# Cross-attention over a memory: one pass over both streams in place of two, with split operands kept in DRAM

## The chip, the cores and the metric

The kernel runs on one core of a Trainium2 chip. The metric is device time in microseconds (us) of one execution. TensorE (PE) does matmuls, VectorE (DVE) and ScalarE (ACT) the elementwise work, GpSimd (POOL) a little of it, and SyncE (SP) issues most DMAs; ACT issues some. SP and ACT each have a DMA queue, and each engine works through its own instructions in order.

## The reference, cut to what matters

```python
D_MODEL = 1024; SEQ = 256; DEC_SEQ = 512; N_MEM = 256; XA_HEADS = 4; XA_HEAD_DIM = 256

def memory_cross_attention(x, mem, w_q, w_kv, w_o):
    B, T, _ = x.shape
    M = mem.shape[1]
    q = (x @ w_q).reshape(B, T, XA_HEADS, XA_HEAD_DIM)
    k, v = jnp.split(mem @ w_kv, 2, axis=-1)
    k = k.reshape(B, M, XA_HEADS, XA_HEAD_DIM)
    v = v.reshape(B, M, XA_HEADS, XA_HEAD_DIM)
    s = jnp.einsum('bthd,bmhd->bhtm', q, k).astype(jnp.float32) * (XA_HEAD_DIM ** -0.5)
    p = jax.nn.softmax(s, axis=-1).astype(v.dtype)
    o = jnp.einsum('bhtm,bmhd->bthd', p, v).reshape(B, T, D_MODEL)
    return o @ w_o
# one layer: x = LN0(a*x + 0.5*SwiGLU_1(x)); x = LN1(a*x + mixer(x));
#            x = LN2(a*x + memory_cross_attention(x, mem)); x = LN3(a*x + 0.5*SwiGLU_2(x))
```

It is done for two streams with the same weights: S ("sample"), 512 tokens, and P ("prompt"), 256 tokens, each with a memory of its own of 256 rows.

## The kernel before

All arithmetic is float32. Every operand of a matmul is split into a high and a low part (`split`: ACT copies the source to `hi`, DVE computes `lo = src - hi`), and a product is three matmuls: hi x hi, hi x lo, lo x hi. `load_w` brings 128 x 1024 of a weight into one of three `raw` buffers by SP's queue and splits it into one of five `wh`/`wl` pairs.

The stages are: first feed-forward, mixer, cross-attention, second feed-forward. The mixer ends with the merge: products with w_gla_out (`pt<-oT,wh`), gated and added up on DVE (`sig`, `t`), and split into `xh`/`xl`. Then `tok_out` multiplies with w_mix_out, 48 matmuls of 512 columns (`to`) for two token tiles and one half of the columns, and adds into `acc`, the residual in SBUF (128 x 6 token tiles x 1024); `norm` is the layer norm on DVE; `to_T` transposes `acc` on PE (`lt`) and splits it into `xh`/`xl`.

Cross-attention is done stream after stream by a `Cross` object, with 33 buffers of 128 x 512 ("units"). `keys_values` is a generator; `fill(ns)` takes steps from it between the `to_T` calls and `drain` takes the rest. K has 256 columns a matmul (one stream), V 512. `attend` goes through the heads: the query projections (`pt<-xh,wh`, 512 columns for S and 256 for P) stand between the scores (`sc`), softmax (`mx`, `e`, `sm`), transposes of the probabilities (`pT`) and the products with V (`ov`). `project` multiplies with w_xo. The weights w_xk, w_xv, w_xq and w_xo are loaded and split for each stream.

The feed-forwards use seven products in place of eight for a pair of weight blocks (`seven`, `products`): the input is held as quarters A11 to A22 and sums S1 to S4 of them (`sums`, on DVE), the weight blocks are summed too, and each of the seven products has 12 matmuls of 384 columns, in the accumulators `px`, `py`, `pz`.

A scheduler places what the Python code records: engines' queues come out in an order of its own, within what buffers and pools allow. A tile's buffers are set by `bufs`; a load into a buffer waits until its last reader is done.

Of the kernel before, what the change touches and what calls it, by code (L numbers as in the profile page):

```python
# [14 lines left out]
D = 1024  # L15
NK = 8
# [8 lines left out]
UNITS = 33  # L25
WARM = 8
LO_K = (5, 7)
LO_V = (1, 3)
# [5 lines left out]
FILL = (14000, 14000, 8000, 14000)  # L34
# [24 lines left out]
def _encoder(ctx, tc, nc, io, out, dbg):  # L59
# [30 lines left out]
    def load_w(src, lo_eng=None, pool=None, in_parts=False):  # L90

        raw = wp.tile([128, 1024], F32, tag="raw", bufs=3, name=nid("raw"))
        h = (pool or wp).tile([128, 1024], F32R, tag="wh", bufs=1 if pool else 5, name=nid("wh"))
        l = (pool or wp).tile([128, 1024], F32R, tag="wl", bufs=1 if pool else 5, name=nid("wl"))
# [963 lines left out]
    def tok_out(src, groups, lhs, after, alt=False, hooks=()):  # L1058


        hooks = list(hooks)
        for half in range(2):
            ws = []
            for gi, (s, ts) in enumerate(groups):
                pss = [psum(nid("to")) for _ in ts]
                for kp in range(4):
                    if gi == 0:
                        ws.append(load_w(src[kp, half], nc.vector if alt and kp % 2 else None))
                    for x, t in enumerate(ts):
                        tcs = slice(t * 128, (t + 1) * 128)  # L1070
                        for kk in range(2):
                            k = 2 * kp + kk
                            lh, ll = lhs(s, k, tcs)
                            tok_mm(pss[x][:], ws[kp], kk, lh, ll, k == 0, k == NK - 1)
                    if hooks:
                        hooks.pop(0)()
                for x, t in enumerate(ts):
                    add_acc(s, t, half, pss[x][:], True)
                if half == 1:
                    after[gi]()  # L1080
# [5 lines left out]
    class Cross:  # L1086
        def __init__(self, s, ap, bufs):
            self.s, self.ap, self.bufs = s, ap, bufs
            self.Kt, self.V, self.q, self.sc, self.pr, self.oT = [], {}, {}, {}, {}, []

        def unit(self, name, dt=F32R):
            return self.ap.tile([128, 512], dt, tag="u", bufs=self.bufs, name=nid(name))

        def load_mem(self, pin):
            s, unit = self.s, self.unit
            self.mh, self.ml = [], []
            raws = [unit("mraw", F32) for c in range(4)]
            for c in range(4):
                if pin:
                    tc.keep_in_program_order(nc.scalar.dma_start(raws[c][:], io[f"mem{s.name}"][c]))  # L1100
                else:
                    nc.sync.dma_start(raws[c][:], io[f"mem{s.name}"][c])
            for c in range(4):
                a, l = unit("mh"), unit("ml")
                split(a[:], l[:], raws[c][:])
                self.mh += [a[:, 0:256], a[:, 256:512]]
                self.ml += [l[:, 0:256], l[:, 256:512]]

        def keys_values(self):
            s, unit, mh, ml = self.s, self.unit, self.mh, self.ml  # L1110
            for h in range(4):
                ps = psum(nid("K"))
                for b in range(2):
                    w = load_w(io["w_xk"][2 * h + b], nc.vector if (2 * h + b) in LO_K else None)
                    proj_T(w, s, rh=mh, rl=ml, T=256, ps=ps[:, b * 256:(b + 1) * 256])
                    yield 2650
                a, l = unit("Kh"), unit("Kl")
                split(a[:], l[:], ps[:])
                self.Kt.append((a, l))
            for half in range(2):  # L1120
                pss = [psum(nid("V")) for _ in range(2)]
                for kp in range(4):
                    w = load_w(io["w_xv"][kp, half], nc.vector if kp in LO_V else None)
                    for m in range(2):
                        for kk in range(2):
                            k = 2 * kp + kk
                            ms = slice(m * 128, (m + 1) * 128)
                            tok_mm(pss[m][:], w, kk, mh[k][:, ms], ml[k][:, ms], k == 0, k == NK - 1)
                    yield 2600
                for m in range(2):  # L1130
                    a, l = unit("Vh"), unit("Vl")
                    split(a[:], l[:], pss[m][:])
                    self.V[m, half] = (a, l)

        def query(self, h, b):
            s = self.s
            w = load_w(io["w_xq"][2 * h + b], nc.vector if b and s is P else None)
            ps = proj_T(w, s)
            a, l = self.unit("qh"), self.unit("ql")
            split(a[:, :s.T], l[:, :s.T], ps)  # L1140
            self.q[h, b] = (a, l)

        def scores(self, h):
            s = self.s
            kh, kl = self.Kt[h]
            es = []
            for tp in range(s.nt // 2):
                ps = psum(nid("sc"))
                for u in range(2):
                    tcs = slice((2 * tp + u) * 128, (2 * tp + u + 1) * 128)  # L1150
                    for b in range(2):
                        bs = slice(b * 256, (b + 1) * 256)
                        qh, ql = self.q[h, b]
                        mm3(ps[:, u * 256:(u + 1) * 256], qh[:, tcs], ql[:, tcs], kh[:, bs], kl[:, bs],
                            b == 0, b == 1)
                mx = sp.tile([128, 2], F32, tag="mx", name=nid("mx"))
                sm = sp.tile([128, 2], F32, tag="sm", name=nid("sm"))
                nc.vector.tensor_reduce(mx[:], ps[:].rearrange("p (a b) -> p a b", b=256), AX.X, ALU.max)
                nc.vector.tensor_scalar(mx[:], mx[:], -1.0 / 16, None, ALU.mult)
                e = self.unit("e", F32)  # L1160
# [4 lines left out]
                nc.vector.reciprocal(sm[:], sm[:])  # L1165
                for u in range(2):
                    us = slice(u * 256, (u + 1) * 256)
                    nc.vector.tensor_scalar(e[:, us], e[:, us], sm[:, u:u + 1], None, ALU.mult)
                es.append(e)
            self.sc[h] = es  # L1170

        def probs_T(self, h):
            s = self.s
            pr = []
            for m in range(2):
                ps = psum(nid("pT"))
                for t in range(s.nt):
                    c = (t % 2) * 256 + m * 128
                    nc.tensor.transpose(ps[:, t * 128:(t + 1) * 128], self.sc[h][t // 2][:, c:c + 128], ident[:])
                a, l = self.unit("ph"), self.unit("pl")  # L1180
                split(a[:, :s.T], l[:, :s.T], ps[:, :s.T])
                pr.append((a, l))
            self.pr[h] = pr

        def values(self, h):
            s = self.s
            for b in range(2):
                ps = psum(nid("ov"))[:, :s.T]
                es = slice((h % 2) * 256 + b * 128, (h % 2) * 256 + (b + 1) * 128)
                for m in range(2):  # L1190
                    vh, vl = self.V[m, h // 2]
                    ph, pl = self.pr[h][m]
                    mm3(ps, vh[:, es], vl[:, es], ph[:, :s.T], pl[:, :s.T], m == 0, m == 1)
                a, l = self.unit("oh"), self.unit("ol")
                split(a[:, :s.T], l[:, :s.T], ps)
                self.oT.append((a, l))

        def attend(self):
            self.query(0, 0)
            self.query(0, 1)  # L1200
            self.query(1, 0)
            for h in range(4):
                self.scores(h)
                if h < 3:
                    self.query(h + 1, 1)
                if h > 0:
                    self.values(h - 1)
                if h == 0:
                    self.query(2, 0)
                if h < 3:  # L1210
                    self.probs_T(h)
                if h == 1:
                    self.query(3, 0)

        def project(self, after):
            groups = [(self.s, ts) for ts in ((0, 1), (2, 3))[:self.s.nt // 2]]
            tok_out(io["w_xo"], groups, lambda s, k, tcs: (self.oT[k][0][:, tcs], self.oT[k][1][:, tcs]),
                    after, self.s is P, [lambda: self.probs_T(3), lambda: self.values(3)])
# [234 lines left out]
```

## Time and profile before

| | |
|---|---|
| median of 3 timed runs | 1767.03 us (1766.86 to 1767.19) |
| profiled execution | 1769.73 us, span 1767.9 us |
| mean granted clock of PE | 0.997 |
| PE / DVE / ACT / POOL busy | 1756.3 / 1259.6 / 764.4 / 26.0 us |
| DMA | 253.11 MB, mean 143 GB/s |
| first w_mix_out matmul | at 932.27 us |
| first weight of S's K | at 999.25 us |
| last matmul of the old attention | about 1268 us |

The profiled execution took 2.7 us longer than the median of the timed ones; sums are made against it, and then carried to the median. In rows of groups the columns are: line, engine, operation, output <- inputs, shapes and count, then busy time in us, mean duration in ns, and the idle time before them with what ended it. In rows of the order of time: start, duration, engine, line, operation. PE's matmuls overlap, so the time that one takes from the stream is the distance between two starts and not its duration. In rows of a window: window, length, busy us of PE, weight loads, DVE, ACT and POOL, granted clock, DMA share, GB/s. Line numbers are those of the kernel before.

### The profile page before, as it was taken

The page shows a single profiled execution, that of the slowest core. Times are in us where ns is not written, and L with a number is a line of the kernel's source. Part 1 is how long each engine was busy: PE and PEld are TensorE (multiplying, and loading weights), DVE is VectorE, ACT ScalarE, POOL GpSimd, SP SyncE. Part 2 cuts the span into 40 slices and gives each one's busy share as a digit, 9 for nine tenths or more (in the row PEclk, how much of TensorE's full clock was granted, in tenths as well). Part 3 has the DMA queues.
Part 4 walks back from the last instruction along what each step waited for, and adds up shares of the span by engine and source line. Part 5 has one row for each costly group of instructions (what it writes and reads, how often), then busy time and mean ns, then how long its engine had stood idle before and what let it go on. Part 6 is the DMA issues. An engine that isn't in the chain of part 4 may idle for free.

```text
span 1767.9 us, 25206 instructions
## 1 busy us (share of the span) xinstructions
PE 1756.3 (99%) x9758; PEld 1617.2 (91%) x9758; DVE 1259.6 (71%) x2151; ACT 764.4 (43%) x1291; POOL 26.0 (1%) x60
## 2 busy tenths in 40 slices
PE   9999999999999999999999999999999999999998
PEld 9999999988899999888888988899899999998886
DVE  8777777687668554678675965596697777766866
ACT  6444444443235544655232253345344444444431
POOL 0000000000100000000000000000000000000002
PEclk9999999999999999999999999999999999999999
DMA  5433333587333334211364262255423333337951
GB/s 198 141 120 118 123 123 112 203 312 262 134 108 108 132 125 131 95 48 49 116 218 131 83 191 72 84 191 167 155 80 127 114 124 125 129 100 288 336 181 72
DMA packets 100536, 253.11 MB, mean 143 GB/s; under 512 B 10017, under 2 KB 28193, under 8 KB 100417
## 3 DMA queue, kind: packets, MB, share of 16 engines
q1 hardware_dynamic: 92352, 234.73, 39.4%
q10 hardware_dynamic: 8064, 16.78, 2.6%
q8 instruction: 76, 1.25, 0.3%
q14 instruction: 44, 0.35, 0.1%
HBM read 205.07 MB, written 46.40 MB: 142 GB/s over the span
## 4 chain that ended last, share of the span: by engine, by line
PE 96%; DVE 2%; DMA 1%; ACT 0%; issue 0%; SPq 0%; DVEq 0%; ACTq 0%
PE px L475 23%; PE dn L286 13%; PE py L475 11%; PE pz L475 6%; PE pt L106 6%; PE pt L107 6%; PE pt L108 6%; PE to L106 2%; PE to L107 2%; PE to L108 2%; PE dn L107 2%; PE dn L106 2%; PE dn L108 2%; PE pp L475 1%; PE lt L191 1%; PE K L108 1%
## 5 line engine op out<-in xcount | busy, mean ns | idle before, releaser
L87 ACT ACTIVATE wh<-raw 128x512 fp32r<-128x512 f32 (+2 forms) x309 | 256.1, 831 | 314.3 <-PE pt L107 77.5
L88 DVE TENSOR_TENSOR wl<-raw,wh 128x512 fp32r<-128x512 f32 (+2 forms) x309 | 289.1, 938 | 142.6 <-ACT wh L87 141.9
L286 PE MATMUL dn<-wh,ao 128*128 128x512 f32 x600 | 185.5, 389 | 0.0
L106 PE MATMUL pt<-xh,wh 128*128 128x512 f32 (+2 forms) x512 | 173.8, 339 | 0.0
L107 PE MATMUL pt<-xl,wh 128*128 128x512 f32 (+2 forms) x512 | 173.2, 338 | 0.0
L108 PE MATMUL pt<-xh,wl 128*128 128x512 f32 (+2 forms) x512 | 172.7, 337 | 0.0
L286 PEld LDWEIGHTS dn<-wh,ao 128*128 128x128 f32 x600 | 112.6, 188 | 23.5
L87 ACT ACTIVATE wh<-tt 128x512 fp32r<-128x512 f32 x156 | 94.0, 624 | 72.0 <-PE px L475 60.5
L286 PE MATMUL dn<-wl,ao 128*128 128x512 f32 x300 | 116.7, 389 | 0.0
L106 PEld LDWEIGHTS pt<-xh,wh 128*128 128x128 f32 x512 | 97.4, 190 | 9.9 <-issue 0.5
L88 DVE TENSOR_TENSOR wl<-tt,wh 128x512 fp32r<-128x512 f32 x156 | 104.0, 685 | 3.0 <-ACT wh L87 2.2
L107 PEld LDWEIGHTS pt<-xl,wh 128*128 128x128 f32 x512 | 97.6, 191 | 9.0 <-issue 0.3
L108 PEld LDWEIGHTS pt<-xh,wl 128*128 128x128 f32 x512 | 97.5, 190 | 9.1
L552 DVE SCALAR_TENSOR_TENSOR h<-sil,sum 128x384 f32<-128x384 f32 x78 | 43.5, 557 | 54.8 <-ACT sil L551 54.8
L475 PE MATMUL px<-xh,wl 128*128 128x384 f32 x232 | 77.5, 334 | 0.0
L475 PE MATMUL px<-xh,wh 128*128 128x384 f32 x232 | 77.5, 334 | 0.0
L475 PE MATMUL px<-xl,wh 128*128 128x384 f32 x232 | 77.5, 334 | 0.0
L87 ACT ACTIVATE ao<-sr 128x768 fp32r<-128x768 f32 x50 | 41.9, 843 | 67.1 <-issue 24.7
L551 ACT ACTIVATE sil<-sum 128x384 f32<-128x384 f32 x39 | 20.5, 525 | 111.4 <-DVE sum L487 111.4
L286 PEld LDWEIGHTS dn<-wl,ao 128*128 128x128 f32 x300 | 56.3, 188 | 11.7
L480 ACT ACTIVATE snap<-px 128x384 f32<-128x384 f32 x78 | 37.8, 485 | 51.6 <-PE px L475 51.0
L106 PE MATMUL dn<-wh,hr 128*128 128x512 f32 (+1 forms) x150 | 57.7, 385 | 0.0
(372 smaller groups left out, 4712.1 us busy)
## 6 DMA issues: line engine op xcount, KB each, us to landing
raw<-in_ffn_gu_dram SPq DMA_DIRECT2D x84, 512.0 KB, 3.5
raw<-in_ffn_dn_dram SPq DMA_DIRECT2D x64, 512.0 KB, 5.7
raw<-in_w_mix_dram SPq DMA_DIRECT2D x32, 512.0 KB, 3.5
sr<-sspill SPq DMA_DIRECT2D x32, 384.0 KB, 5.2
sspill<-hs SPq DMA_DIRECT2D x56, 192.0 KB, 1.9
hspill<-hq SPq DMA_DIRECT2D x12, 768.0 KB, 3.7
hr<-hspill SPq DMA_DIRECT2D x24, 384.0 KB, 6.3
raw<-in_w_xk_dram SPq DMA_DIRECT2D x16, 512.0 KB, 3.5
```

What stands on the lines that cost most here:

```text
L87: nc.scalar.activation(hi, src, AF.Copy)
L88: (lo_eng or nc.vector).tensor_tensor(lo, src, hi.bitcast(F32), op=ALU.subtract)
L106: nc.tensor.matmul(o, lh, rh, start=start, stop=False)
L107: nc.tensor.matmul(o, lh, rl, start=False, stop=False)
L108: nc.tensor.matmul(o, ll, rh, start=False, stop=stop)
L191: nc.tensor.transpose(ps[:, j * 128:(j + 1) * 128], A[:, c:c + 128], ident[:])
L286: nc.tensor.matmul(ps[t][:], l, r[:, o], start=start and k == 0 and m == 0, stop=stop and k == 1 and m == 2, skip_group_check=True)
L475: nc.tensor.matmul(ps, l[:, c], r[:, k, :], start=st and n == 0, stop=sp_ and n == 2, skip_group_check=True)
L480: ins = nc.scalar.activation(t, ps, AF.Copy)
L551: nc.scalar.activation(sil[:], g, AF.Silu)
L552: ins = nc.vector.scalar_tensor_tensor(h32[:, half * HT:(half + 1) * HT], sil[:], -0.5, u, ALU.mult, ALU.mult)
```

## The change

`attention()` takes the place of `Cross`, its `attend` and `project`.

- The memories of both streams are loaded together, through the three `raw` buffers of the weights, and split into `mh`/`ml` (128 x 8 x 512), before w_mix_out is worked with. K is made for both streams at once (8 blocks of 512 columns), V for four blocks of memory rows.
- K, V and the queries are split and written to DRAM (`kd`, `vd`, `qd`) by ACT's queue; the rows after LN1 go to DRAM too (`x2`), and `acc` serves as scratch space until they are brought back.
- The queries of both streams come from the seven-product scheme: four heads, 7 x 12 matmuls of 384 columns each.
- Heads are then worked off for both streams: `fetch` reads q, k and v of a head from DRAM on SP's queue, into pool `even` (heads 0 and 2) or `odd` (heads 1 and 3), one q and one k buffer in each and two v buffers in `odd`. `odd` opens when the pool of the sums is closed.
- Half of the softmax normalisation goes to POOL. The products with V are split straight into `xh`/`xl`. w_xo is loaded once, and `tok_out` takes a list of tile groups and halves.

```diff
+        mp, sg, lp = opened("mem", "right"), opened("stage"), opened("lnx")
+        for c in range(4):
+            r = wp.tile([128, 1024], F32, tag="raw", bufs=3, name=nid("raw"))
+            for n, s in enumerate(STREAMS):
+                nc.sync.dma_start(r[:, n * 512:n * 512 + 512], io[f"mem{s.name}"][c])
+            split(*[m[:, 2 * c:2 * c + 2, :].rearrange("p k (s t) -> p k s t", s=2) for m in (mh, ml)],
+                  r[:].rearrange("p (s k t) -> p k s t", s=2, k=2))
...
+            for i in range(8):
+                w = load_w(io["w_xk"][i])
+                ps = proj_T(w, None, rh=[mh[:, k, :] for k in range(NK)], rl=[ml[:, k, :] for k in range(NK)], T=512)
+                yield 5500
+                t, h, l = staged()
+                split(h, l, ps)
+                nc.scalar.dma_start(kd[:, i], t[:].bitcast(F32).rearrange("p (a b) -> p a b", a=2))
...
+        def fetch(h, parts):
+            pool = ev if h % 2 == 0 else od
+            for p in parts:
+                if p == "q":
+                    t = pool.tile([128, 2, 2, TT], F32R, tag="q", bufs=1, name=nid("q"))
+                    src = qd[:, 2 * h:2 * h + 2]
+                elif p == "k":
+                    t = pool.tile([128, 2, 2, 512], F32R, tag="k", bufs=1, name=nid("k"))
+                    src = kd[:, 2 * h:2 * h + 2]
+                else:
+                    t = od.tile([128, 4, 2, 256], F32R, tag="v", bufs=2, name=nid("v"))
+                    src = vd[:, h]
+                nc.sync.dma_start(t[:].bitcast(F32), src)
+                tl[p, h] = t
+
+        fetch(0, "k")
+        qs = opened("qs", "right")
+        for h in range(4):
+            g1, x, u1, u2 = products(ws)
+            for b, parts in ((1, (u1, u2)), (0, (g1, x))):
+                t = qs.tile([128, 2, TT], F32R, tag="qst", bufs=2, name=nid("qst"))
...
+                nc.scalar.dma_start(qd[:, 2 * h + b], t[:].bitcast(F32))
...
+            if h == 1:
+                fetch(0, "q")
+        stack["qs"].close()
+        stack["sums"].close()
+        od = opened("odd")
+        fetch(1, "qk")
+        fetch(0, "v")
...
+                V.reciprocal(sm[:], sm[:])
+                nc.gpsimd.tensor_scalar(e[:, 0:256], e[:, 0:256], sm[:, 0:1], None, ALU.mult)
+                V.tensor_scalar(e[:, 256:512], e[:, 256:512], sm[:, 1:2], None, ALU.mult)
...
+        scores(0, S)
+        scores(0, P)
+        for h in range(3):
+            scores(h + 1, S)
+            probs_T(h, S)
+            scores(h + 1, P)
+            if h < 2:
+                fetch(h + 2, "qk")
+            fetch(h + 1, "v")
+            probs_T(h, P)
+            values(h, S)
+            values(h, P)
...
+        tok_out(io["w_xo"], [a + (0,), b + (0,), a + (1,), b + (1,), c + (0,), c + (1,)], merged,
+                {2: [ln3(*a)], 3: [ln3(*b)], 4: [lambda: [to_T(S, t) for t in range(4)]], 5: [ln3(*c)]},
+                [[lambda: probs_T(3, S), lambda: probs_T(3, P)], [lambda: values(3, S), lambda: x2_back((0, 1))],
+                 [lambda: values(3, P)], [reopen]], lambda: late["pool"])
```

Where instructions stand, at the two places of which the prediction speaks. First ACT's queue at the end of the merge (`xh<-t` are the merge's last splits, `wh` a weight's split, `mh` a memory block's), before:

```order
749 L87 ACTIVATE xh<-t_8056 128x256
750 L87 ACTIVATE xh<-t_8057 128x512
751 L87 ACTIVATE wh_8955<-raw_8954 128x1024
752 L87 ACTIVATE xh<-t_8057 128x256
753 L87 ACTIVATE xh<-t_8058 128x512
754 L87 ACTIVATE xh<-t_8058 128x256
755 L87 ACTIVATE mh_8748<-mraw_8740 128x512
```

and now:

```order
748 L84 ACTIVATE xh<-t_8058 128x512
749 L84 ACTIVATE xh<-t_8058 128x256
750 L84 ACTIVATE mh<-raw_8749 128x1024
751 L84 ACTIVATE mh<-raw_8754 128x1024
752 L84 ACTIVATE mh<-raw_8759 128x1024
753 L84 ACTIVATE mh<-raw_8764 128x1024
754 L84 ACTIVATE wh_8780<-raw_8779 128x1024
```

Before, `wh_8955` is the fifth split of w_mix_out, all five ahead of the merge's end; now the first of them, `wh_8780`, stands behind the four memory blocks. SP's queue there, before (`sig` are the merge's gates):

```order
258 L96 DMA raw_8828<-in_w_mix_out_dram 128x1024
259 L1009 DMA sig_8581<-sigd 128x768
260 L96 DMA raw_8954<-in_w_mix_out_dram 128x1024
261 L1009 DMA sig_8617<-sigd 128x768
262 L1009 DMA sig_8659<-sigd 128x768
263 L1009 DMA sig_8695<-sigd 128x768
264 L96 DMA raw_8972<-in_w_mix_out_dram 128x1024
```

and now:

```order
264 L1006 DMA sig_8695<-sigd 128x768
265 L150 DMA ln_g_8769<-in_ln_g_dram 128x512
266 L150 DMA ln_g_8771<-in_ln_g_dram 128x512
267 L150 DMA ln_b_8773<-in_ln_b_dram 128x512
268 L1102 DMA raw_8764<-in_memS_dram 128x512
269 L1102 DMA raw_8764<-in_memP_dram 128x512
270 L150 DMA ln_b_8775<-in_ln_b_dram 128x512
271 L93 DMA raw_8779<-in_w_mix_out_dram 128x1024
```

The first w_mix_out load, `raw_8779`, has moved behind all gates and behind the fourth memory block; three memory blocks hold the three `raw` buffers, so the fourth block and then `raw_8779` wait for the first and second `ml` on DVE.

Second, the place between head 0 and head 1. PE before, at the end of the scores of head 0 of S:

```order
5549 L107 MATMUL sc_10052<-Kl_9437,qh_9972 128x256
5550 L108 MATMUL sc_10052<-Kh_9436,ql_9973 128x256
5551 L106 MATMUL pt_10081<-xh,wh_10076 128x512
5552 L107 MATMUL pt_10081<-xl,wh_10076 128x512
5553 L108 MATMUL pt_10081<-xh,wl_10077 128x512
```

and now, at the end of head 0 of P (k_10045 and q_10318 are head 0's, k_10565 and q_10563 head 1's):

```order
5845 L104 MATMUL sc_10615<-k_10045,q_10318 128x256
5846 L105 MATMUL sc_10615<-k_10045,q_10318 128x256
5847 L103 MATMUL sc_10638<-k_10565,q_10563 128x256
5848 L104 MATMUL sc_10638<-k_10565,q_10563 128x256
5849 L105 MATMUL sc_10638<-k_10565,q_10563 128x256
```

A query projection stood there; now head 1's scores follow at once. SP's queue for these loads, now (q_10720 and k_10722 are head 2's, v_10567 head 0's):

```order
320 L93 DMA raw_11288<-in_w_xo_dram 128x1024
321 L1305 DMA acc<-x_8734 128x1024 x2
322 L1212 DMA q_10720<-qd 128x3072
323 L1212 DMA q_10563<-qd 128x3072
324 L1212 DMA k_10565<-kd 128x2048
325 L1212 DMA v_10567<-vd 128x2048
326 L1212 DMA k_10722<-kd 128x2048
327 L1212 DMA v_10724<-vd 128x2048
328 L1212 DMA q_10856<-qd 128x3072
```

None of these loads existed before. q of head 2 goes into the buffer of head 0's q, and stands ahead of q and k of head 1.

More of the change, by code (lines that the diff above doesn't have):

```diff
@@ L1056, in mixer, with tok_out @@
         mo.close()
[L1058 to L1076, printed above, removed]
-                for x, t in enumerate(ts):
-                    add_acc(s, t, half, pss[x][:], True)
-                if half == 1:
-                    after[gi]()
+    def tok_out(src, order, lhs, after, hooks=(), more=None):
+        hooks, ws = list(hooks), {}
+        for gi, (s, ts, half) in enumerate(order):
+            pss = [psum(nid("to")) for _ in ts]
+            for kp in range(4):
+                if (kp, half) not in ws:
+                    ws[kp, half] = load_w(src[kp, half], pool=more() if more and len(ws) >= 5 else None, extra=3)
+                for x, t in enumerate(ts):
+                    tcs = slice(t * 128, (t + 1) * 128)
+                    for kk in range(2):
+                        k = 2 * kp + kk
+                        lh, ll = lhs(s, k, tcs)
+                        tok_mm(pss[x][:], ws[kp, half], kk, lh, ll, k == 0, k == NK - 1)
+                if hooks:
+                    for f in hooks.pop(0):
+                        f()
+            for x, t in enumerate(ts):
+                add_acc(s, t, half, pss[x][:], True)
+            for f in after.get(gi, ()):
+                f()
@@ L1143, in scores @@
[L1143 to L1146, printed above, removed]
+                            tok_mm(pss[m][:], w, kk, mh[:, k, ms], ml[:, k, ms], k == 0, k == NK - 1)
+                    yield 5450
+                for m in range(4):
+                    t, h, l = staged()
+                    split(h, l, pss[m][:])
+                    t3 = t[:].bitcast(F32).rearrange("p (a h c) -> p a h c", a=2, h=2)
+                    for u in range(2):
+                        nc.scalar.dma_start(vd[:, 2 * half + u, m], t3[:, :, u, :])
@@ new lines, in norms, with f, ln_params @@
+        def norms(s, ts, i, gb, dst):
+            def f():
+                for t in ts:
+                    norm(s, t, gb, i)
+                    nc.sync.dma_start(dst[:, s.t0 + t, :], glob["acc"][:, s.t0 + t, :])
+            return f
+        def ln_params(pool, i):
+            return load_ln(lambda nm: pool.tile([128, 512], F32, tag="gb", bufs=4, name=nm), i)
+        pending.append(keys_values())
+        gb = ln_params(lp, 1)
+        groups = [(S, (0, 1)), (S, (2, 3)), (P, (0, 1))]
+        tok_out(io["w_mix_out"], [g + (half,) for half in range(2) for g in groups], merged,
+                {3 + n: [norms(s, ts, 1, gb, x2)] for n, (s, ts) in enumerate(groups)})
@@ new lines, in attention, with ring, get @@
+        to_T(S, 0)
+        to_T(S, 1)
+        fill(FILL[0])
+        to_T(S, 2)
+        to_T(S, 3)
+        fill(FILL[1])
+        to_T(P, 0)
+        to_T(P, 1)
+        stack["lnx"].close()
+        X = {}
+        sp_ = opened("sums")
+        for nm in ("S1", "S2", "S4"):
+            X[nm] = tuple(sp_.tile([128, 4, HT], F32R, name=f"q{nm}{p}") for p in "hl")
+        quarters(X)
+        X["S3"] = X.pop("A21")
+        flat = glob["acc"][:].rearrange("p a b -> p (a b)")
+        def ring(offs, n):
+            turn = [0]
+            def get():
+                turn[0] += 1
+                o = offs[turn[0] % len(offs)]
+                return flat[:, o:o + n]
+            return get
@@ new lines, in attention @@
+        snap_t = ring([2048 + n * HT for n in range(4)], HT)
+        sum_t = ring([3584 + n * HT for n in range(3)], HT)
+        x0_t = ring([0, TT, 4736], TT)
+        _, weights_of, _, products, _ = seven(X, sg, 1, ring([n * 512 for n in range(4)], 512), snap_t, sum_t)
+        for k in range(4):
+            fill(FILL[2])
+            a = []
+            for q in (k, k + 4):
+                x = x0_t()
+                V.tensor_tensor(x, xh["all"][:, q, :].bitcast(F32), xl["all"][:, q, :].bitcast(F32), op=ALU.add)
+                a.append(halves(x))
+            last_sum = sums(X, (snap_t, sum_t), k, *a)
@@ new lines, in attention @@
+        fill(FILL[2])
+        wq = io["w_xq"]
+        ws = weights_of(wq[0], wq[1])
+        marks["dve"] = last_sum
+        drain()
+        stack["mem"].close()
+        ev, od = opened("even", "right"), None
+        tl = {}
+        def fetch(h, parts):
[12 more added lines that the diff above has]
+                tl[p, h] = t
@@ L1177, in probs_T @@
                 for t in range(s.nt):
[L1178 to L1186, printed above, removed]
+                    c = t * 256 + m * 128
+                    nc.tensor.transpose(ps[:, t * 128:(t + 1) * 128], es[h, s][:, c:c + 128], ident[:])
@@ L1194, in values @@
[L1194 to L1218, printed above, removed]
+                    mm3(ps, v[:, m0 + m, 0, c], v[:, m0 + m, 1, c], p[:, m, 0, :], p[:, m, 1, :], m == 0, m == 1)
+                split(xh[s.name][:, 2 * h + b, :], xl[s.name][:, 2 * h + b, :], ps)
@@ new lines, in attention, with x2_back, reopen @@
+        scores(0, S)
[10 more added lines that the diff above has]
+            values(h, P)
+        def x2_back(ts):
+            for t in ts:
+                nc.sync.dma_start(glob["acc"][:, t, :], x2[:, t, :])
+        late = {}
+        def reopen():
+            for nm in ("odd", "even"):
+                stack[nm].close()
+            late["pool"] = opened("late")
+            late["gb"] = ln_params(late["pool"], 2)
+            x2_back(range(2, 6))
```

176 lines of the change are left out of this document (60 added, 116 removed).

## The prediction

> **What bounds the kernel now.** I read the page's busy times and its chain first, then what TensorE (PE) waits for, then the stretch that the change replaces.
>
> ```profile
> PE 1756.3 (99%) x9758; PEld 1617.2 (91%) x9758; DVE 1259.6 (71%) x2151; ACT 764.4 (43%) x1291; POOL 26.0 (1%) x60
> PE 96%; DVE 2%; DMA 1%; ACT 0%; issue 0%; SPq 0%; DVEq 0%; ACTq 0%
> PE warm L75 <- POOL ident masks.py:199: 2.3, 1, 2.3
> PE o L934 <- DVE st L919: 1.1, 1, 1.1
> PE sc L108 <- DVE ql L88: 0.3, 1, 0.3
> 932.27:1270.00 337.73, 337.44 (x1916) 296.82 (x1915) 225.07 (x452) 133.03 (x217) 0.00 (x0) 1.00 0.41 134
> ```
>
> PE is busy 99% of the span and is 96% of the chain that ends last. The three rows of its waits are all that it has in the whole kernel. The last row is the stretch from the first w_mix_out matmul to the end of the old attention: 337.44 of 337.73 us busy, at full clock, while DVE has 225 and ACT 133. So matmuls taken out here are worth their full time, work for other engines is free as long as it comes in time, and every new wait of PE is paid in full.
>
> **The matmuls.** Counts from the groups of 930 to 1310 us by shape; steps (start to start) from the order of time and the chain:
>
> ```profile
> L106 PE MATMUL K<-mh,wh 128*128 128x256 f32 x128 | 36.5, 285 | 0.0
> L106 PE MATMUL pt<-xh,wh 128*128 128x512 f32 x96 | 37.6, 391 | 0.0
> L106 PE MATMUL pt<-xh,wh 128*128 128x256 f32 x96 | 27.2, 284 | 0.0
> 1002.93 0.28 PE L106 MATMUL K<-mh,wh 128*128 128x256 f32 x1
> 1004.73 0.28 PE L106 MATMUL K<-mh,wh 128*128 128x256 f32 x1
> 331.90 114.67 PE dn L286 x504
> 53.18 4.16 PE px L475 x24
> ```
>
> The durations overlap, so the step counts: the two K rows stand 15 matmuls apart, 1.80/15 = 0.120 us for 256 columns; 114.67/504 = 0.2275 for 512; 4.16/24 = 0.1733 for the 384 columns of a seven-product matmul. Each group has three lines of equal count. Of the 96 in each pt group 64 are the queries, 32 the second feed-forward, which stays. Removed: K 384 x 0.120 = 46.1; queries 192 x 0.2275 = 43.7 and 192 x 0.120 = 23.0; together 112.8. Added: K for both streams at once, 192 x 0.2275 = 43.7; queries by seven products, 4 heads x 7 x 12 = 336 x 0.1733 = 58.2; together 101.9. PE loses **10.9 us** of work; V, scores, transposes, values, w_xo keep theirs. The 0.3 us wait goes too: -11.2.
>
> xk, xv, xq and xo are now loaded and split once instead of twice; ACT and DVE lose that work, which PE covered, so it is worth nothing here. Sums for the seven products, staging of K and V, and their stores to DRAM come in: DVE had 113 us free in the stretch, and a product block of 84 x 0.1733 = 14.6 us asks of it some twenty operations of about 0.55 us. I cost these at nothing; if DVE fell behind there, PE would wait at the reuse of a product's bank.
>
> **The wait at the start.** Before, five of the eight w_mix_out weights were loaded during the merge, and the first `to` followed without a gap:
>
> ```profile
> 932.15 0.28 PE L108 MATMUL pt<-oT,wl 128*128 128x256 f32 x1
> 932.27 0.40 PE L106 MATMUL to<-wh,xh 128*128 128x512 f32 x1
> 929.68 1.22 DVE L88 TENSOR_TENSOR wl<-raw,wh 128x1024 fp32r<-128x1024 f32 x1
> 934.59 0.42 ACT L87 ACTIVATE xh<-t 128x256 fp32r<-128x256 f32 x1 [0.30 <-DVE t L1037]
> L87 ACT ACTIVATE wh<-raw 128x1024 fp32r<-128x1024 f32 x74 | 78.5, 1061 | 159.1 <-PE to L108 58.5 <-PE pt L107 28.7 <-DVE acc L172 23.5
> L88 DVE TENSOR_TENSOR wl<-raw,wh 128x1024 fp32r<-128x1024 f32 x76 | 92.6, 1220 | 70.9 <-ACT wh L87 70.5
> raw<-in_w_mix_out_dram SPq DMA_DIRECT2D x8, 512.0 KB, 4.0
> raw<-in_ffn_dn_dram SPq DMA_DIRECT2D x64, 512.0 KB, 5.7
> x<-acc SPq DMA_DIRECT2D x12, 512.0 KB, 2.6
> ```
>
> Now the four memory blocks take the three `raw` buffers, in front of every w_mix_out load, and their splits stand on ACT and DVE behind the merge's last split. The first weight's buffer is free only after the second `ml`. The chain: the last xh split starts about 1.1 us earlier than its row, as the weight split at 929.68 is no longer ahead on DVE, and ends at 933.9. mh to 935.0; two ml of 1.13 (1.22 overlapped) to 937.3; the load is issued and lands after 4.0: 941.3; wh to 942.4; wl to 943.5. PE has ended at 932.4 and can do two matmuls of 0.23 before wl: it waits **10.6 us**. With landings of 2.6 and 5.7 us from the other rows it is 9.2 to 12.3. The following weights land at least as fast as PE uses them.
>
> **The wait for head 1.** On SP the q of head 2 stands ahead of q and k of head 1. Pool `even` has one q buffer, so that load waits for the last scores matmul of head 0 (P), and everything behind it on the queue waits too. PE's next instruction is the first score of head 1. So PE stands still while q2, q1 and k1 move: 128 x 3072 x 4 = 1.57 MB twice, 128 x 2048 x 4 = 1.05 MB: 4.2 MB. What else moves then: the four loads of w_xo and x2 issued in the 5.5 us before (2.1 MB) and 0.8 MB of queries stored then, of which 5.5 x 0.371 = 2.0 has moved, so 0.9 MB is left; and 0.8 MB of the last queries on their way out: 5.9 MB. The rate, from windows where the queue is full:
>
> ```profile
> 1610.00:1620.00 10.00, 10.00 (x46) 8.29 (x45) 4.28 (x4) 2.88 (x3) 0.00 (x0) 1.00 1.03 371
> 355.00:360.00 5.00, 5.00 (x24) 4.14 (x23) 3.15 (x4) 2.44 (x3) 0.00 (x0) 1.00 1.05 394
> 940.00:945.00 5.00, 5.00 (x23) 4.13 (x22) 4.04 (x7) 2.53 (x4) 0.00 (x0) 1.00 0.89 276
> ```
>
> The last column is GB/s. Landing has a fixed part: 2.6 us for 0.52 MB, less 0.52/0.371 = 1.4, leaves 1.2. So 5.9/0.371 + 1.2 = **17.1 us**. Ends: 4.2/0.394 + 1.2 = 11.9 with nothing else in the way, 5.9/0.276 + 1.2 = 22.6 at the slowest of the three windows. I take the value from the fullest long window. The v, k and q loads behind come every 3 to 6 us, while a head takes PE 9.7 us, so no second wait follows.
>
> **The clock after each wait.** After the one longer wait that before has (1.1 us at 854.6, in a stretch of small matmuls):
>
> ```profile
> 855.00:860.00 5.00, 4.27 (x30) 2.77 (x30) 4.81 (x12) 1.43 (x3) 0.00 (x0) 0.79 0.02 3
> 860.00:865.00 5.00, 5.00 (x16) 3.79 (x16) 3.60 (x13) 1.65 (x3) 0.00 (x0) 0.53 0.60 194
> 862.04 0.63 PE L107 MATMUL pt<-xl,wh 128*128 128x512 f32 x1
> 862.47 0.63 PE L108 MATMUL pt<-xh,wl 128*128 128x512 f32 x1
> ```
>
> the granted clock was 0.79 and 0.53, and a 512-column step took 0.43 instead of 0.23. From 860.6 to 864.6 that lost 1.9 us; over both windows 5 x 0.21 + 5 x 0.47 = 3.4. Two waits, 2.0 each: **+4**, ends 0 and 6.8. The Trainium skill ("TensorE: Matmul & The Clock Gate", section "What's actually happening") says that an idle window of about 3.4 us throttles to half and some 3.4 us of sustained work releases it: an estimate of 1.7 a wait, 3.4 in place of 4. The rows agree on half speed, but show it after a wait of only 1.1 us, which that rule does not give; the sum keeps the rows.
>
> **The small waits.** In each head the chain from scores to `pT` and to `ov` has to fit beside 9.7 us of PE:
>
> ```profile
> L1163 ACT ACTIVATE e<-sc,mx 128x256 f32<-128x256 f32 x24 | 11.1, 471 | 19.9 <-DVE mx L1159 17.4 <-PE ov L108 2.4
> L1168 DVE TENSOR_SCALAR e<-e,sm 128x256 f32<-128x256 f32 x24 | 7.4, 351 | 0.4
> L175 POOL TENSOR_TENSOR acc<-acc,ln_b 128x512 f32<-128x512 f32 x14 | 18.6, 1359 | 1400.8 <-ACT acc L174 1400.8
> L172 DVE SCALAR_TENSOR_TENSOR acc<-acc,mv,ln_g 128x512 f32<-128x512 f32 x24 | 17.7, 741 | 0.0
> ```
>
> No query projection stands between these steps any more, and half of the normalisation moves from DVE (0.35) to POOL, whose nearest row is 1.36 for twice the columns. I take 0.25 a head, **+1**, ends 0 and 3. At the end, the transposes of the LN3 rows come right behind one block of 48 w_xo matmuls (10.9 us), in which DVE has two tiles of layer norm, 8 operations of about 0.7, beside four weight splits of 1.2: **+1**, ends 0 and 5.
>
> **Sum:** -11.2 + 10.6 + 17.1 + 4 + 1 + 1 = +22.5. The profiled execution took 1769.7 us (span 1767.9), so a profile of after should show about 1792. The median of the timed runs stands 2.7 lower, at 1767.0: 1789.5.
>
> **Rivals.** (1) Only one of the two large waits is there, because loads run ahead of where I place them: without the start's, -11.2 + 17.1 + 2 + 2 = +10, 1777; without head 1's, +3.4 or so, 1770. For it: DMA is only 0.41 busy in the stretch. Against: both stand on the order of one queue, which no idle DMA engine changes. (2) Fetches from the new DRAM blocks are much slower than weights, their rows lying 32 or 48 KB apart per partition: at half of 371 GB/s the wait is 5.9/0.186 + 1.2 = 33, and the time 1805; nothing in this trace reads such rows at that size, for or against, though 276 GB/s beside 0.89 busy shows a slower mix. The Trainium skill ("DMA: Bandwidth & Descriptors", "Latency and other measured facts") tells of 207 GB/s at a 512 KB pitch, none measured below; that would estimate 5.9/0.207 + 1.2 = 30, and no row here shows it. (3) Faster: large transfers move so fast that head 1's wait nearly goes, and the matmul saving decides. With the start at its least (9.2), no slow clock and no small waits, it takes -11.2 + 9.2 + w below -3.5, hence w below zero for a measurable gain; even w = 0 gives 1765. So the start wait would have to fall too, to under 7.7 us, which needs the first load to land in 1.1 us. No row has that.
>
> **Chances.** Within 0.2% (3.5 us) this kernel cannot be told from no change. My forecast with both waits 0.70; rival 1 0.11, of which 0.03 ends within 0.2%; rival 2 0.10; rival 3, with what I may have misread in the order, 0.09, of which 0.07 faster and 0.02 same. Slower is 0.70 + 0.08 + 0.10 = 0.88, same 0.05, faster 0.07. Range: the low ends give -11.2 + 9.2 + 11.9 = +9.9, 1777; the high ends -11.2 + 12.3 + 22.6 + 6.8 + 3 + 5 = +38.5, 1805. I give 1776 to 1805.
>
> **What would show it.** Right: PE waits of about 10 us at the first `to` for wh or wl of w_mix_out, and about 17 us at the first `sc` of head 1 for its q and k; 240 matmuls fewer (768 out, 528 in); a granted clock near 0.5 for some us behind both; steps of 0.173 in the queries. Wrong: product steps above 0.18 or gaps between blocks (DVE as bound); a start wait under 5; k1 landing within 8 us; or gaps in every head that add up to more than 5.

## The result and the profile after

The changed kernel is slower: 1798.27 us, the median of 4 runs (1797.28 to 1800.41), against 1766.94 for the kernel before (4 runs, 1766.57 to 1767.19). The ratio is 1.0179, with a 95% interval of 1.0161 to 1.0197, or +31.3 us. The profiled execution took 1797.84 us, its span 1796.1.

First the page of the kernel after: busy time, share of the span and number of instructions of each engine, and the shares of the chain that ended last.

```profile
PE 1751.1 (97%) x9518; PEld 1607.2 (89%) x9518; DVE 1267.2 (71%) x2191; ACT 753.8 (42%) x1303; POOL 38.7 (2%) x72
PE 92%; DVE 3%; DMA 3%; ACT 1%; issue 1%; SPq 0%; ACTq 0%; DVEq 0%
```

PE has the 240 matmuls fewer and 5.2 us less busy time, and yet the span is 28.2 us longer. PE's share of the chain is down from 96% to 92%, and DVE's and DMA's are up from 2% and 1% to 3% each. So the time lies in waits; these are PE's, in the kernel after (us in total, times, longest), but for the 2.3 us at the program's start, which both kernels have:

```profile
PE sc L103 <- DMA k<-kd: 17.4, 1, 17.4
PE to L103 <- ACT wh L84: 14.3, 1, 14.3
PE py L472 <- ACT acc L477: 1.6, 1, 1.6
PE o L931 <- DVE st L916: 1.1, 1, 1.1
PE py L472 <- ACT snap L477: 0.3, 1, 0.3
```

The two large ones are new, and each happens once. The first stands at the first score of head 1, the second at the first w_mix_out matmul. The 1.6 at `py` lies in the queries; the 0.3 for `snap` lies at 46.6 us, in the first feed-forward, and has no part in the change.

**The start.** The order of time of the kernel after, SP's rows (start, duration), then ACT's, then PE's:

```profile
933.62 0.33 SPq L1102 DMA_DIRECT2D raw<-in_memS_dram  x1
933.99 0.43 SPq L1102 DMA_DIRECT2D raw<-in_memP_dram  x1
934.47 0.43 SPq L150 DMA_DIRECT2D ln_b<-in_ln_b_dram  x1
934.99 1.22 SPq L93 DMA_DIRECT2D raw<-in_w_mix_out_dram  x2
```

```profile
936.98 1.06 ACT L84 ACTIVATE mh<-raw 128x1024 fp32r<-128x1024 f32 x1 [2.76 <-DMA raw<-in_memP_dram]
942.44 1.06 ACT L84 ACTIVATE wh<-raw 128x1024 fp32r<-128x1024 f32 x1 [4.40 <-DMA raw<-in_w_mix_out_dram]
```

```profile
943.55 1.22 PE L103 MATMUL to<-wh,xh 128*128 128x512 f32 x2 [14.28 <-ACT wh L84]
944.81 0.80 PE L104 MATMUL to<-wl,xh 128*128 128x512 f32 x1
946.25 0.63 PE L104 MATMUL to<-wl,xh 128*128 128x512 f32 x1
949.62 0.39 PE L104 MATMUL to<-wl,xh 128*128 128x512 f32 x1
```

The load of the first weight is issued at 934.99 and its split starts on landing, at 942.44: 7.4 us. Ahead of it on the queue stand the last memory block and a row of layer-norm parameters, spread to all partitions. PE's matmuls last 0.63 behind the wait and 0.39 some 6 us later: that is the granted clock going from half to full.

**Head 1.** SP's rows, then PE's, in the order of time of the kernel after:

```profile
1171.74 0.82 SPq L1212 DMA_DIRECT2D q<-qd  x2
1172.61 0.49 SPq L1212 DMA_DIRECT2D k<-kd  x1
1174.52 0.32 SPq L1212 DMA_DIRECT2D v<-vd  x1
```

```profile
1189.10 0.55 PE L103 MATMUL sc<-k,q 128*128 128x256 f32 x1 [17.39 <-DMA k<-kd]
1191.58 0.41 PE L105 MATMUL sc<-k,q 128*128 128x256 f32 x1
```

The first row of SP's is two loads, the q of head 2 and the q of head 1; PE had ended at 1171.7, and stands still until k has landed. What the DMA engines did in both waits show windows of the kernel after (window, length, busy us of PE, weight loads, DVE, ACT and POOL, granted clock, DMA share, GB/s):

```profile
936.00:938.00 2.00, 0.00 (x0) 0.00 (x0) 0.00 (x0) 1.02 (x1) 0.00 (x0) 0.50 0.85 186
1180.00:1185.00 5.00, 0.00 (x0) 0.00 (x0) 0.00 (x0) 0.00 (x0) 0.00 (x0) 0.50 1.01 428
```

At head 1 nothing at all works but the DMA engines, at 428 GB/s. At the start they are 0.85 busy and move 186.

**The ledger.** From PE's starts, for the stretch from the end of the merge's matmuls to the second feed-forward's first `pp` (us); the rows are its larger parts, not all. `fixed` is experiment 5, below.

| part | before | after | `fixed` |
|---|---|---|---|
| gap before the first `to` | 0 | 14.4 | 0 |
| w_mix_out, 288 matmuls | 65.3 | 68.4 | 65.3 |
| K | 46.3 | 45.1 | 44.2 |
| V | 43.8 | 45.0 | 44.8 |
| queries | 66.8 | 60.2 | 60.3 |
| scores, waits in them included | 18.1 | 36.4 | 17.5 |
| products with V, waits included | 16.7 | 18.0 | 20.3 |
| the whole stretch | 370.5 | 401.8 | 367.5 |

The stretch is 31.3 us longer, as much as the timed difference. The spans of the two profiles differ by 3.1 less, since the profiled execution of before lost that much to half clock in 855 to 865 us, far ahead of the change.

### The profile page after: what moved, and what is told of

Same layout as the page of the kernel before. It is cut to its first block, busy times and chain, and to the rows that moved or that the text cites. A ratio compares the mean times of both kernels' runs of the same rounds, so it can differ in the third digit from the quotient of the medians.

```text
span 1796.1 us, 24825 instructions
## 1 busy us (share of the span) xinstructions
PE 1751.1 (97%) x9518; PEld 1607.2 (89%) x9518; DVE 1267.2 (71%) x2191; ACT 753.8 (42%) x1303; POOL 38.7 (2%) x72
## 4 chain that ended last, share of the span: by engine, by line
PE 92%; DVE 3%; DMA 3%; ACT 1%; issue 1%; SPq 0%; ACTq 0%; DVEq 0%
PE px L472 24%; PE dn L283 13%; PE py L472 12%; PE pz L472 6%; PE pt L103 5%; PE pt L104 5%; PE pt L105 5%; PE to L103 3%; PE to L104 2%; PE to L105 2%; PE dn L103 2%; PE dn L104 2%; PE dn L105 2%; PE pp L472 1%; DMA k<-kd 1%; PE lt L188 1%
## 5 line engine op out<-in xcount | busy, mean ns | idle before, releaser
L84 ACT ACTIVATE wh<-raw 128x512 fp32r<-128x512 f32 (+2 forms) x281 | 221.0, 789 | 280.4 <-PE to L105 91.0
L85 DVE TENSOR_TENSOR wl<-raw,wh 128x512 fp32r<-128x512 f32 (+2 forms) x281 | 249.1, 889 | 105.2 <-ACT wh L84 104.9
L103 PE MATMUL pt<-xh,wh 128*128 128x512 f32 (+2 forms) x384 | 129.9, 338 | 0.0
L104 PE MATMUL pt<-xl,wh 128*128 128x512 f32 (+2 forms) x384 | 129.3, 337 | 0.0
L105 PE MATMUL pt<-xh,wl 128*128 128x512 f32 (+2 forms) x384 | 128.9, 336 | 0.0
L103 PE MATMUL to<-wh,xh 128*128 128x512 f32 x192 | 76.1, 397 | 14.3 <-ACT wh L84 14.3
L105 PEld LDWEIGHTS pt<-xh,wl 128*128 128x128 f32 x384 | 72.7, 189 | 6.4
L104 PEld LDWEIGHTS pt<-xl,wh 128*128 128x128 f32 x384 | 72.7, 189 | 6.3 <-issue 0.2
L104 PE MATMUL to<-wl,xh 128*128 128x512 f32 x192 | 75.9, 395 | 0.0
L105 PE MATMUL to<-wh,xl 128*128 128x512 f32 x192 | 75.7, 394 | 0.0
```

The costliest lines, as they stand in the source:

```text
L84: nc.scalar.activation(hi, src, AF.Copy)
L85: (lo_eng or nc.vector).tensor_tensor(lo, src, hi.bitcast(F32), op=ALU.subtract)
L103: nc.tensor.matmul(o, lh, rh, start=start, stop=False)
L104: nc.tensor.matmul(o, lh, rl, start=False, stop=False)
L105: nc.tensor.matmul(o, ll, rh, start=False, stop=stop)
```

## The experiments

The theory is that the two large waits are made by the order of SP's queue and by the few buffers behind it, that both are paid in full, and that they add. The rivals are that a wait taken away comes back behind it (the loads being late by bandwidth and not by order), and that the rest of the loss lies in the new steps themselves, the products' sums or the split K and V. In the sessions of the experiments the kernel before had medians of 1766.86 and 1766.81. Line numbers differ a little from kernel to kernel; in those with the pinned loads they stand two or more higher.

### 1. The memory blocks loaded later

```diff
-        for c in range(4):
-            r = wp.tile([128, 1024], F32, tag="raw", bufs=3, ...)
-            ... # load both memories into r, split into mh, ml
+        def mem_block(c): ... # the same, as a function
...
         tok_out(io["w_mix_out"], ...,
-                {3 + n: [norms(...)] ...})
+                {3 + n: [norms(...)] ...},
+                [[], [], [], []] + [[mem_block(c)] for c in range(4)])
```

> Edit to the changed kernel: the four memory blocks are loaded and split during the second group of w_mix_out (after its first four weights), not in front of it. Theory A (the start wait is the memory blocks in the raw buffers ahead of w_mix_out): the 14.4 us wait at the first to, the 0.8 us for its low part and the 2.2 us at half clock go, no wait takes their place, 1798.3 - 17.4 = 1781. Rival B (DVE or ACT is the limit at the end of the merge in any case, or K's fill then waits for the memory): 1790 or more, with a new wait of 8 us or more at the first to or at the first K matmul.

Measured: 1781.38 us (1780.74 to 1783.71), ratio 1.0085 [1.007, 1.01], 16.9 less than the kernel after. PE's larger waits in it:

```profile
PE sc L103 <- DMA k<-kd: 16.6, 1, 16.6
PE py L472 <- ACT acc L477: 1.5, 1, 1.5
PE o L931 <- DVE st L916: 1.1, 1, 1.1
```

The wait at `to` is gone, and its half clock with it, and none of more than 0.4 us has come in its place; K starts as early as it is wanted. The memory blocks had no business in front of the weights.

### 2. The fetches in the order of the program

```diff
-                nc.sync.dma_start(t[:].bitcast(F32), src)          # fetch
+                tc.keep_in_program_order(nc.sync.dma_start(t[:].bitcast(F32), src))
```

The loads of `x2` back into `acc` and the last five of w_xo are held to the program's order in the same way.

> Edit to the changed kernel: the DMAs of the heads' q, k, v, of the x2 rows and of the last five w_xo weights keep the order in which the code records them, so that q and k of head 1 go in front of q of head 2 and of what was prefetched ahead of them. Same bytes, same buffers. Theory A (the 17.4 us wait is the order on SP's queue): q1 and k1 are issued in the last product block, land before head 0's scores end, wait under 1 us, and the 1.2 us at half clock goes too: 1798.3 - 18.6 = 1780. Rival B (the transfers themselves are too slow, whatever their order): the wait stays at 8 us or more or moves to head 2's scores: 1789 or more.

Measured: 1780.43 us (1779.21 to 1781.83), 1.0078 [1.0063, 1.0093], 17.8 less than the kernel after. Some of SP's rows in it, and those of PE's waits that are at the start and in the heads:

```profile
1154.70 0.32 SPq L1214 DMA_DIRECT2D q<-qd  x1
1158.52 0.32 SPq L1214 DMA_DIRECT2D k<-kd  x1
1160.60 0.32 SPq L1214 DMA_DIRECT2D v<-vd  x1
1169.53 0.32 SPq L1214 DMA_DIRECT2D q<-qd  x1
```

```profile
PE to L105 <- ACT wh L84: 13.5, 1, 13.5
PE ov L106 <- DVE p L85: 0.8, 2, 0.6
PE sc L105 <- DMA k<-kd: 0.3, 1, 0.3
```

Head 1's q and k are issued at 1154.7 and 1158.5 and no longer after 1171.7, because the q of head 2 (here at 1169.5), which has to wait for head 0, now stands behind them. The wait of 17.4 is down to 0.3, and that one belongs to a later head. In this kernel the same bytes move beside PE's work; its window, with the same columns as above:

```profile
1180.00:1185.00 5.00, 4.65 (x41) 4.48 (x39) 2.97 (x8) 1.92 (x8) 0.22 (x1) 1.00 1.04 442
```

So bandwidth was not what made the fetch late.

### 3. The memory operands 32 bytes lower

In K and V a 512-column step takes longer than the 0.2275 us of the weights' matmuls. `mh` began at byte 196576 of a partition; a pad ahead of its pool moves it to 196544, a multiple of 64.

```diff
+        pad = opened("pad", "right").tile([128, 8], F32, name="pad")
+        nc.vector.memset(pad[:], 0.0)
```

> Edit to the changed kernel: 32 bytes are reserved ahead of the memory pool, so that mh and ml start at a multiple of 64 bytes in a partition (and q, k of the even heads too); before they start 32 bytes off. Theory A (K and V matmuls take 0.2345 us instead of 0.2275 because of the start address): step back to 0.2275, 384 x 0.007 = 2.7 us less, 1795.6. Rival B (it comes from the shape of the tile, from DMA traffic or from DVE and ACT at work beside): step stays, 1798.3.

Measured: 1796.01 us (1794.4 to 1797.1), 1.0165 [1.0148, 1.0182]. The order of time, the first and the last of the first 72 matmuls of K, of the kernel after and then of this one:

```profile
1013.65 0.48 PE L103 MATMUL pt<-mh,wh 128*128 128x512 f32 x1
1030.31 0.39 PE L105 MATMUL pt<-mh,wl 128*128 128x512 f32 x1
```

```profile
1010.99 0.48 PE L103 MATMUL pt<-mh,wh 128*128 128x512 f32 x1
1027.34 0.40 PE L105 MATMUL pt<-mh,wl 128*128 128x512 f32 x1
```

16.66/71 = 0.2346 became 16.35/71 = 0.2303; for V, where `mh` and `ml` are the other operand, 192 matmuls went from 44.97 to 44.79 us. K and V together take 1.0 us less. This is no spread between executions: all K matmuls take 45.06 us in each of the four profiles without the pad and 44.25 in each of the five with it. The rest of the 2.3 us lies elsewhere. In this profile the first weight landed 5.8 us after its issue and not 7.4, though the queue has the same order; the start wait was 12.8 instead of 14.3, and the half clock behind it cost 1.1 less, while behind head 1's wait it cost 1.3 more. Whether the pad has a part in that was not tried. So the start address explains rather more than half of K's longer step and little of V's.

### 4. The layer-norm parameters later

```diff
-        gb = ln_params(lp, 1)
+                {2: [lambda: late_gb.append(ln_params(lp, 1))], ...
```

> Edit to the changed kernel: the layer norm parameters are loaded later, so that the last of them (0.25 MB, one row for all partitions) no longer stands in front of the first w_mix_out weight on SP's queue, but behind two of them. Theory A (that load makes the weight land 7.4 us after its issue where 4.0 was used in the forecast): landing near 4 to 5, start wait 14.4 down to 11 to 12, 1795.5. Rival B (the memory blocks just ahead, in rows of 2 KB, and the second weight beside it make it slow): landing stays above 6.5, time within 1 us of 1798.3.

Measured: 1796.53 us (1796.23 to 1797.69), 1.017 [1.0155, 1.0185]. Its rows on SP and on ACT, and its waits:

```profile
934.41 1.46 SPq L93 DMA_DIRECT2D raw<-in_w_mix_out_dram  x2
935.92 0.42 SPq L150 DMA_DIRECT2D ln_b<-in_ln_b_dram  x1
939.02 1.06 ACT L84 ACTIVATE wh<-raw 128x1024 fp32r<-128x1024 f32 x1 [1.35 <-DMA raw<-in_w_mix_out_dram]
```

```profile
PE sc L103 <- DMA k<-kd: 18.0, 1, 18.0
PE to L103 <- ACT wh L84: 10.9, 1, 10.9
```

With the parameter row behind the weight, the weight lands in 4.6 us instead of 7.4, and the wait is 10.9 instead of 14.3, as expected. With the row ahead of it the weight landed after 7.1 us in experiment 2 and 5.8 in experiment 3, so by these profiles the row is worth 1.2 to 2.8 us. The time fell by 1.7 only, because the scores of the heads lost 1.7 again: 0.6 in the wait for k, the rest in the clock. Windows of this kernel, whose wait for k ended at 1186.3, and of the kernel after, where it ended at 1189.1:

```profile
1190.00:1192.00 2.00, 2.00 (x12) 2.00 (x11) 0.33 (x2) 1.02 (x4) 0.00 (x0) 0.50 0.89 369
1192.00:1194.00 2.00, 2.00 (x19) 2.00 (x19) 1.38 (x3) 0.97 (x5) 0.00 (x0) 1.00 1.00 418
```

Here the clock is still at half 3.7 to 5.7 us after the wait; in the kernel after it is full from 2.9 us on.

### 5. The three together

> The edits of mem_later, fetch_first and pad32 together. Theory A (both large waits are matters of order alone and independent, the matmul saving is there below them): 1798.3 - 17.4 (start) - 18.6 (head 1) - 1.5 (K and V) = 1761, 6 us or 0.3% under before. Rival B (one wait was hiding another, for instance head 2's fetches or a late w_xo weight, which now comes out): 1766 or more, with a new wait of PE of 4 us or more after head 0.

This kernel has the edits of 1, 2 and 3. Measured: 1764.09 us (11 runs, 1763.09 to 1767.37), 0.9982 [0.9973, 0.9991] against 1766.81. Its larger waits in the stretch, and the one at `o` ahead of it:

```profile
PE py L474 <- ACT acc L479: 1.7, 1, 1.7
PE ov L106 <- DVE p L85: 1.2, 3, 0.6
PE o L933 <- DVE st L918: 1.1, 1, 1.1
PE sc L105 <- DMA k<-kd: 0.5, 1, 0.5
```

Both large waits are gone at once. The single edits save 16.9, 17.8 and, in K and V, 1.0; 1798.27 less these is 1762.6, and 1764.1 was measured, so they add to within 1.5 us. The version is 2.7 us faster than the kernel before. It falls 3 us short of what was expected. Of this, 2.3 lie in the products with V, which the ledger has at 18.0 in the kernel after and at 20.3 here (they took 19.7 in experiment 2 already), and 0.5 in K and V, which saved 1.0 and not 1.5. Once k is there in time, PE meets the splits of the probabilities (the row `ov`, 1.2) and, right behind the products of head 0, k of head 2 (0.5); the rest is short pauses whose cause stays open.

### 6. The queries without the seven products

```diff
-            g1, x, u1, u2 = products(ws)
-            ...
+            for b in range(2):
+                w = load_w(wq[2 * h + b])
+                for s in STREAMS:
+                    c = slice(s.off, s.off + s.T)
+                    split(t[:, 0, c], t[:, 1, c], proj_T(w, s))
```

The quarters and sums of the input are left out too.

> Like fixed, but the queries are projected in the plain way, 512 and 256 columns a matmul, and the sums for the seven products are left out. Theory A (the seven products save what their matmuls save, 66.8 - 58.2, and lose 1.9 in a wait at their start): fixed + 7. Rival B (sums and added weight blocks cost PE elsewhere, so that the scheme saves nothing here): fixed + 2 or less.

Measured: 1768.7 us (1768.34 to 1769.24), 1.001 [1.0001, 1.0018]: 4.6 more than `fixed`, between the 7 of theory A and the 2 of rival B. By PE's starts the queries take 66.7 us in place of 60.3, so the seven products are worth 6.4 there, wait at their start included, and about 1 us of it is lost again in the heads. The saving of the matmuls is real, and the sums are hidden but for that wait. The staging of K and V is in both kernels, so this does not price it.

### 7. All of the normalisation on DVE

```diff
-                nc.gpsimd.tensor_scalar(e[:, 0:256], ...)
+                V.tensor_scalar(e[:, 0:256], ...)
```

> Like fixed, but all of the softmax normalisation is on DVE, none on POOL, where one took 1.06 us against 0.35. Theory A (the small waits before the products with V, 1.3 us over the heads, come from the chain through POOL): 0.5 to 1.5 less than fixed. Rival B (they come from ACT's exponentials and splits; POOL's half lies beside them): within 0.5 of fixed, or more, since DVE has more to do.

Measured: 1763.01 us (12 runs, 1762.61 to 1769.22), 0.9982 [0.9974, 0.9991]. The median is 1.1 under `fixed`, but the intervals of the ratio overlap almost wholly: undecided. Its waits in the heads are 0.9 and 0.2 where `fixed` had 1.2:

```profile
PE ov L106 <- DVE p L85: 0.9, 2, 0.5
PE ov L105 <- ACT p L84: 0.2, 1, 0.2
```

By PE's starts the first three heads' products with V take 6.1, 4.4 and 4.4 us, against 6.6, 4.6 and 5.0. So at most about 1 us of the heads' loss is POOL's.

### 8. The memory operands another 1 KB lower

```diff
-        pad = opened("pad", "right").tile([128, 8], F32, name="pad")
+        pad = opened("pad", "right").tile([128, 264], F32, name="pad")
```

> Like fixed, but with 1056 bytes in place of 32 ahead of the memory pool: the start stays a multiple of 64 and moves down by 1 KB. Theory A (beyond the offset in 64 bytes the step of the K and V matmuls, 0.2304 and 0.2333 after pad32, depends on where in SBUF mh and ml lie): a K or V step differing by 0.002 or more. Rival B (what is left comes from something else, as the tile's layout or what runs beside): both steps as in pad32.

Measured: 1763.69 us (1763.34 to 1765.54), 0.9984 [0.9975, 0.9993]. K's first 72 matmuls take 16.59 us from the first to the start of what follows, and V's 192 take 44.79, the same as in experiment 3. A shift by 1 KB that keeps the multiple of 64 changes nothing; why K and V stay at 0.230 and 0.233 and not at 0.2275 is open.

## Why the prediction was right or wrong

It had the sign, both waits, their places and their causes, and the time lies within its range; the value is 8.8 us too low.

| term | forecast | measured |
|---|---|---|
| matmuls | -11.2 | -6.9 |
| wait at the start | +10.6 | +15.2 |
| wait for head 1 | +17.1 | +17.4 |
| clock behind the two waits | +4 | +3.4 |
| heads and LN3 | +2 | +1.9 |
| sum | +22.5 | +31.0 |

The ledger's stretch is 31.3 us longer; the 0.3 between is not assigned to a term.

**The matmuls** failed in "K for both streams at once, 192 x 0.2275 = 43.7" and in "V, scores, transposes, values, w_xo keep theirs": the steps of K and V were 0.235 and 0.234, so that K saves 1.2 us where 2.4 were forecast, and V costs 1.2 more. Experiment 3 traces 1.0 of these 2.4 to the start address. The other 1.9 of the 4.3 lie in the queries, 1.6 of them in PE's wait at `py` in their first product block, which "I cost these at nothing" had left out. The prediction feared DVE there, at the reuse of a product's bank; it is ACT that is late:

```profile
1113.97 0.60 ACT L84 ACTIVATE stg<-V 128x512 fp32r<-128x512 f32 x1 [3.64 <-DMA vd<-stg]
1115.00 0.44 PE L472 MATMUL py<-qS4h,wh 128*128 128x384 f32 x1 [1.56 <-ACT acc L477]
```

ACT stands still for 3.6 us, because it has to put the last piece of V into one of two staging buffers and the store of an earlier piece has not landed; the copy that frees the product's bank (`acc<-py`) stands behind that on ACT's queue. It is a third wait of the same kind as the large ones, and every version with the products has it (1.5 to 1.8 us). No experiment takes it away. The queries' 0.173 steps and the hidden sums were right (experiment 6).

**The wait at the start** failed in "the load is issued and lands after 4.0". It landed after 7.4, and even the high end, 5.7, was too short. The 4.0 was the median of eight w_mix_out loads that took 3.4 to 8.8 us by the landings in the trace of before; here a memory block and the parameter row stood ahead on the same queue, and in experiment 4, with that row behind it, the weight landed after 4.6. Of the 4.6 us that the forecast is short, 3.4 are the landing; another 1.0 is the issue, which came 5.9 us after the merge's last matmul and not 4.9. The mechanism, four blocks in three shared buffers ahead of the weights, was right (experiment 1). The 15.2 are 14.4 for wh and 0.8 for wl between the first matmuls, both of which the chain had.

**The wait for head 1** was right in size only because two errors cancel. Windows of the kernel after, of the 5.7 us ahead of the wait and of the wait:

```profile
1166.00:1171.70 5.70, 5.70 (x43) 5.50 (x41) 4.85 (x9) 2.32 (x5) 0.00 (x0) 1.00 0.75 198
1171.70:1189.00 17.30, 0.01 (x1) 0.00 (x0) 2.44 (x9) 2.57 (x12) 2.94 (x3) 0.59 1.00 422
```

The engines moved 422 GB/s and not 371, but 17.3 x 0.422 = 7.3 MB and not 5.9. By the sizes of the DMA packets in the trace (12 KB for q, 8 KB for k and v, 6 KB for the stores of the queries, 4 KB for the rest) these are 4.2 MB of q2, q1 and k1, 1.5 of the last two stores of the queries, 1.0 of w_xo and x2, and 0.6 of the v behind k1. So what failed is "of which 5.5 x 0.371 = 2.0 has moved": ahead of the wait the engines ran at 198 GB/s, and 1.1 MB had moved. The mechanism, a load that waits for a buffer and holds up the urgent ones, was right (experiment 2).

**The clock** cost 2.2 us behind the first wait and 1.2 behind the second, from the steps at 0.5. The 3.4 estimated from the Trainium skill ("TensorE: Matmul & The Clock Gate", "What's actually happening") came out as a sum, and not as two equal parts. That the sum came out is in part luck: over the five profiles with a large wait, the half clock lasted from 2.8 to 6.2 us beyond the end of it.

**The rivals.** Only one large wait: fell. Experiments 1 and 2 are its two cases, at 1781 and 1780 where it had 1777 and 1770; the terms missed above are most of that, the larger landing time all the more in the second. Slow fetches: fell, 428 to 442 GB/s with 32 or 48 KB between partitions' rows. Faster: not in this kernel, but experiment 5 is that case, with both waits taken away by order alone, and it needed both, as the prediction's condition for it said.

## What to carry to other kernels

On a kernel that one engine bounds, read the in-order queues at each border between stages before counting the instructions saved: what stands ahead of the first load that the engine needs, and what does that wait for? Here 7 us were saved in matmuls and 33 us lost to two waits, because loads that nobody needed yet stood ahead of urgent ones, in shared buffers or waiting for a buffer, and moving or pinning these turned +31 into -3. The landing time to use for an urgent load is that of a load with the same neighbours on its queue, not the median, and it has a range: with the same order on the queue it was 5.8 to 7.4 us here.

## What the runs showed of the hardware that was not expected

- Behind a one-row parameter load that is spread over 128 partitions, a load of 0.5 MB on the same queue landed in 7.4, 7.1 and 5.8 us (the kernel after, experiments 2 and 3), and in 4.6 with that row behind it (experiment 4). In the kernel after the DMA engines were 0.85 busy meanwhile, at 186 GB/s.
- Fetches of 8 to 12 KB per partition ran at 428 to 442 GB/s. The Trainium skill ("DMA: Bandwidth & Descriptors", "Where 436 GB/s comes from") says that for transfers between memory and SBUF the memory's share of about 358 GB/s binds, a memory stack's rate divided by two cores, and has 435 as the ceiling of the fabric. With one core at work the measured rates are past the first and about at the second.
- The step of K's matmuls depends on where `mh` and `ml` start: 0.2346 us at 32 bytes off a multiple of 64, 0.2303 at a multiple, and no change for a further 1 KB (experiments 3 and 8).
- The same multiplication by a column of scalars took POOL three times as long as DVE, whose 0.351 the prediction shows (the profiler's spans on POOL are rough); the group in the kernel after:

```profile
L1266 POOL TENSOR_SCALAR e<-e,sm 128x256 f32<-128x256 f32 x12 | 12.7, 1063 | 394.8 <-DMA acc<-x 359.9 <-DVE sm L1265 34.9
```

- The wait of 1.1 us at `o` is in every version, but the half clock behind it is in two of the ten profiles only, those of before and of `fixed`. Windows of `fixed` and of the kernel after:

```profile
860.00:865.00 5.00, 5.00 (x16) 3.76 (x15) 3.81 (x14) 1.41 (x3) 0.00 (x0) 0.54 0.77 210
```

```profile
860.00:865.00 5.00, 5.00 (x29) 4.35 (x28) 4.33 (x16) 1.07 (x2) 0.00 (x0) 1.00 0.71 194
```

The Trainium skill ("TensorE: Matmul & The Clock Gate", "What's actually happening") has an activity window of 3413 ns that is free-running, so that the point of a transition varies. The traces agree: in each of the ten, the granted clock changes at whole multiples of 3.413 us from its first change, and the half clock lasted 6.83 us here and 13.65, 17.07 or 20.48 us around the large waits. They do not agree with an idle window of 3.4 us as the condition: 1.1 us of wait in a stretch of small matmuls was enough. In these two profiles such a window begins within 0.1 us of the start of the wait, in the other eight none begins within 0.3 us of it; that is a hint and not a test. The half clock costs some 3 us, as much as `fixed` gains: its profiled execution took 1767.37 us and its median 1764.09, so that execution alone would have shown no gain.
